# Token projections as Strassen products in a phase of their own

## The chip, the cores and the metric

The kernel runs on one core of a Trainium2 chip. The metric is the device time of one execution in microseconds; less is better.

## The reference

One layer of a gated encoder over two groups of tokens, 256 and 2048, 2304 in all, of width 1024. Normalised tokens go through one wide product with w_in; three branches (pooling, Fourier, attention into 256 memory tokens) are gated, projected, merged and projected once more.

```python
xn = rmsnorm(x, norm_in[l])
mn = rmsnorm(mem, norm_mem[l])
pv, pg, fv, fg, q, ag, mg = split_cols(xn @ w_in[l])
ya = (pool_mixer(pv, w_pool_grp[l], pool_scale[l]) * jax.nn.silu(pg)) @ w_pool_out[l]
yb = (fourier_mixer(fv, w_four_grp[l]) * jax.nn.silu(fg)) @ w_four_out[l]
yc = (memory_xattn(q, mn, w_kv[l]) * jax.nn.silu(ag)) @ w_attn_out[l]
ga, gb, gc = jnp.split(jax.nn.sigmoid(mg + b_gate[l]), N_BRANCH, axis=-1)
merged = ga * ya + gb * yb + gc * yc
x = x + merged @ w_o[l]
```

The pooling mixer takes, for each of four groups of features, the mean over a window of 2, 4, 8 or 16 tokens less the token itself. All is float32.

## The kernel before

Every product is made of three matmuls (SPLITS): each float32 operand is split into a high part (a cast on ACT, L88) and a low part (a subtraction on DVE, L89), and high x high, high x low and low x high are added in PSUM. A weight tile (128 features wide) is loaded as raw by the SP queue and split into hl; four raw and three hl buffers.

Features lie on partitions, tokens along the free dimension. The 2304 tokens are three blocks of 768, a block two halves of 384. First a phase normalises and transposes the tokens (nine chunks of 256), writes them split to DRAM (xs_d), folds w_pool into w_in, and computes the Fourier values pfv; then come the Fourier mixer along tokens, and keys and values of the memory (pv L607, pk L625, stored to kv_d). From 266 us on the main pass goes block by block. It holds the block's split tokens in eight xn tiles, loaded on the POOL queue (L587), and runs in this order on PE:

- pF: the eight tiles of q and ag, with the four heads' attention woven between their matmuls: scores ps, softmax on DVE and ACT (L724 to L732), transposes pt, values po.
- for each of eight output tiles a gate pgc and yc's product pyc, then pfg (four), then pgb and pyb in turn; a gate's sigmoid is on ACT, its multiplication on DVE, and the addition of branch b to partial on POOL (L846).
- ppv and ppg in turn for eight tiles: a pooling value goes to a buffer U, DVE adds shifted copies (L872, L876), corrects the sequence's edges (L881), scales and subtracts (L882), multiplies by the gate (L891) and splits za. Two tiles have each of the four windows.
- pga and pya in turn (L664 is the one matmul line of all these), the sum in partial, its split m, and the output projection pwo (L936) with the residual and the final normalisation (L941, L946).

Each token projection (pF, pfg, ppv, ppg and the three gates: 52 tiles of a block) is 8 x 3 x 2 = 48 matmuls. A projection's closing work on ACT and DVE runs while PE does the next one. In the last block the last tile of the output is closed in two halves. Order on an engine is the order in which a timing model of the framework placed the instructions; POOL's order is the order of the code.

## Time and profile before

| | |
|---|---|
| time, median of 3 runs | 2257.05 us (2256.16 to 2260.65) |
| the profiled execution, its span | 2258.0 us |
| PE busy | 2230.9 us, 99% |
| DVE, ACT, POOL busy | 39%, 29%, 8% |
| main pass | 266 to 2250 us |
| bytes moved | 249.49 MB, 110 GB/s on the mean |

The span runs from the first to the last instruction. Matmuls overlap, so that their busy time adds up to more than the time they take; the chain that ended last shows the time of a run of them. The granted clock is TensorE's share of its full 2.4 GHz.

### The profile page before, as it was taken

Reading aid. Unit: us, or ns where it says so; the run is one execution under the profiler, and the core shown is the slowest. Engines: PE = TensorE matmul, PEld = TensorE weight load, DVE = VectorE, ACT = ScalarE, POOL = GpSimd, SP = SyncE. Lnnn points to the kernel's source line nnn. Section 1 sums busy time; section 2 is a strip of 40 time slices with the busy share of each in tenths; the row PEclk is TensorE's granted clock in tenths of the full one; section 3 lists DMA queues with packets and bytes.
Section 4 is the critical chain, followed back from the end, with each engine's and each line's share of the span. In section 5 each row is a group of like instructions: output and inputs, shape, how many; then the busy total and the mean of one; then the engine's idle time right before and its main releaser. Section 6 shows DMA issues by size and latency. Waiting matters only on the chain.

```text
span 2258.0 us, 30415 instructions
## 1 busy us (share of the span) xinstructions
PE 2230.9 (99%) x13023; PEld 2182.3 (97%) x13023; DVE 886.8 (39%) x1203; ACT 663.6 (29%) x953; POOL 191.5 (8%) x259
## 2 busy tenths in 40 slices
PE   8998999999999999999999999999999999999998
PEld 7998899999999998999999999998999999999996
DVE  6638352223345225552232344235642222343243
ACT  5433252131223114442222222123441222222131
POOL 1226210001100000100012100000000012000000
PEclk9999999999999999999999999999999999999999
DMA  9986931222222225711322222227412312122221
GB/s 327 344 219 226 291 101 52 70 85 66 75 64 67 66 66 195 241 47 57 96 64 68 77 66 57 65 93 259 144 47 66 94 57 83 57 66 62 60 103 75
DMA packets 295338, 249.49 MB, mean 110 GB/s; under 512 B 8644, under 2 KB 264164, under 8 KB 294948
## 3 DMA queue, kind: packets, MB, share of 16 engines
q1 hardware_dynamic: 243552, 171.47, 25.1%
q0 software_dynamic: 50880, 74.20, 11.3%
q8 instruction: 102, 1.67, 0.3%
q10 hardware_dynamic: 772, 1.88, 0.3%
q14 instruction: 32, 0.26, 0.0%
HBM read 201.91 MB, written 45.61 MB: 110 GB/s over the span
## 4 chain that ended last, share of the span: by engine, by line
PE 97%; DVE 1%; DMA 1%; issue 0%; ACT 0%; POOL 0%; SPq 0%; DVEq 0%; ACTq 0%
PE ppv L664 9%; PE ppg L664 9%; PE pgc L664 9%; PE pgb L664 9%; PE pga L664 9%; PE pF L664 9%; PE pya L664 9%; PE pwo L936 9%; PE pfv L316 5%; PE pfg L664 4%; PE pyb L664 4%; PE pyc L664 4%; PE po L756 1%; PE ps L714 1%; PE pv L607 1%; PE pk L625 1%
## 5 line engine op out<-in xcount | busy, mean ns | idle before, releaser
L89 DVE TENSOR_TENSOR hl<-raw,hl 128x1024 fp32r<-128x1024 f32 (+1 forms) x270 | 316.3, 1172 | 589.3 <-ACT hl L88 583.1
L88 ACT CAST hl<-raw 128x1024 fp32r<-128x1024 f32 (+1 forms) x270 | 261.8, 970 | 369.1 <-PE pya L664 136.9
L664 PE MATMUL pF<-xn,hl 128*128 128x384 f32 x1152 | 211.6, 339 | 0.0
L664 PE MATMUL ppv<-xn,hl 128*128 128x392 f32 (+2 forms) x1152 | 208.3, 340 | 0.0
L664 PE MATMUL ppg<-xn,hl 128*128 128x384 f32 x1152 | 205.9, 337 | 0.0
L664 PE MATMUL pgb<-xn,hl 128*128 128x384 f32 x1152 | 205.8, 337 | 0.0
L664 PE MATMUL pgc<-xn,hl 128*128 128x384 f32 x1152 | 205.8, 337 | 0.0
L664 PE MATMUL pga<-xn,hl 128*128 128x384 f32 x1152 | 205.8, 337 | 0.0
L664 PEld LDWEIGHTS ppv<-xn,hl 128*128 128x128 f32 x1152 | 204.6, 188 | 0.0
L664 PE MATMUL pya<-za,hl 128*128 128x384 f32 x1152 | 203.3, 334 | 0.0
L664 PEld LDWEIGHTS ppg<-xn,hl 128*128 128x128 f32 x1152 | 202.3, 188 | 0.0
L664 PEld LDWEIGHTS pgb<-xn,hl 128*128 128x128 f32 x1152 | 202.2, 188 | 0.0
L664 PEld LDWEIGHTS pgc<-xn,hl 128*128 128x128 f32 x1152 | 202.2, 188 | 0.0
L664 PEld LDWEIGHTS pga<-xn,hl 128*128 128x128 f32 x1152 | 202.2, 188 | 0.0
L664 PEld LDWEIGHTS pF<-xn,hl 128*128 128x128 f32 x1152 | 201.1, 188 | 0.3
L664 PEld LDWEIGHTS pya<-za,hl 128*128 128x128 f32 x1152 | 200.3, 188 | 0.0
L936 PE MATMUL pwo<-hl,m 128*128 128x512 f32 x648 | 148.2, 389 | 0.0
L936 PEld LDWEIGHTS pwo<-hl,m 128*128 128x128 f32 x648 | 121.6, 188 | 25.3
L846 POOL TENSOR_TENSOR partial<-partial,gb 128x768 f32<-128x768 f32 x24 | 62.3, 2595 | 766.7 <-ACT hl L88 515.8
L316 PE MATMUL pfv<-xhi,fvw 128*128 128x256 f32 x576 | 107.7, 287 | 0.0
L664 PE MATMUL pyb<-zb,hl 128*128 128x384 f32 x576 | 104.0, 335 | 0.0
L664 PE MATMUL pyc<-zc,hl 128*128 128x384 f32 x576 | 103.9, 335 | 0.0
(240 smaller groups left out, 2364.5 us busy)
## 6 DMA issues: line engine op xcount, KB each, us to landing
raw<-in_w_in_dram SPq DMA_DIRECT2D x136, 512.0 KB, 3.9
raw<-in_w_o_dram SPq DMA_DIRECT2D x40, 512.0 KB, 3.4
xn<-xs_d POOLq DMA_DIRECT2D x16, 776.0 KB, 11.6
...
```

What stands on the lines that cost most here:

```text
L88: nc.scalar.copy(hi, src)
L89: nc.vector.tensor_sub(lo, src, hi.bitcast(F32))
L316: nc.tensor.matmul(o, lhsT=fvw[:, g, a, d * P:(d + 1) * P], rhs=hl[b][:, d, :], start=(d == 0 and s == 0), stop=(d == 7 and s == 2))
L607: nc.tensor.matmul(pv[m // 2][:, m % 2, :], lhsT=mn(a, d)[:, m * P:(m + 1) * P], rhs=w[:, c, k * 512:(k + 1) * 512], start=(d == 0 and s = ...
L625: nc.tensor.matmul(ps[:, 0, :], lhsT=w[:, a, d * P:(d + 1) * P], rhs=mn(c, d), start=(d == 0 and s == 0), stop=(d == 7 and s == 2))
L664: nc.tensor.matmul(ps[:, j, :n], lhsT=w[:, a, d * P:(d + 1) * P], rhs=rhs(c, d, c0, n), start=(d == 0 and s == 0), stop=(d == nd - 1 and s ...
L714: nc.tensor.matmul(flat(ps)[:, t * 256:(t + 1) * 256], lhsT=qT[h][:, a, tt * P:(tt + 1) * P], rhs=kload[h, req(tt)][:, c, :], start=(s == ...
L756: nc.tensor.matmul(ps[:, hf, c0:c0 + n], lhsT=vload[h, r][:, a, m, :], rhs=z[:, c, m * H + c0:m * H + c0 + n], start=(m == 0 and s == 0), ...
L846: nc.gpsimd.tensor_add(partial[:, c, :], partial[:, c, :], sg[:, :TB])
L936: nc.tensor.matmul(ps[:, hf, :], lhsT=m[d][:, a, lc:lc + P], rhs=w[:, cc, hf * 512:(hf + 1) * 512], start=(d == 0 and (a, cc) == (0, 0)), ...
```

## The change

The 52 projection tiles of a block are taken two at a time. A pair of 128-feature tiles and the two halves of the 1024 inputs make a 2 x 2 matrix of weight blocks (A11 to A22); the 256 tokens of a chunk are two groups of 128, so that the tokens make 2 x 2 blocks too. Seven products of sums of such blocks replace the eight of the plain form. A product has 4 x 3 matmuls of 384 columns, in which the moving operand is 128 tokens from each of three chunks.

The seven token operands of a block (xo0 to xo6, 1.57 MB each with both parts) are read from DRAM (xq_d) on the POOL queue. For the first block's three chunks the normalising phase makes them (x_sums); for the other six it stores the transposed tokens (xr_d), and x_prep makes them within the first phase, in pairs 6, 12 and 18 of blocks 0 and 1. Each operand has one buffer: at the last pair of a block it is loaded anew after its last product. Weight sums S1 to S4 are made on DVE, split, and kept in ten buffers; PE's order is written by hand, preparing eight products ahead.

All results (q, ag, fg, pv, pg and the gates, after silu or sigmoid) are stored to DRAM on the POOL queue, two of 0.39 MB per pair. When all three blocks are done, a second phase goes over the blocks again and loads them on the SP queue into five shared buffers (ld_tile). It begins with the attention of block 0; attention of the next block is taken into the loop over ya. The closing of the last tile in halves is dropped, and every block loads w_o twice.

```diff
+    pairs = [((wp_d, c * P, "pv", c), (wp_d, (c + 4) * P, "pv", c + 4)) for c in range(4)]
+    pairs += [((w_in, Q0 + h * P, "q", h), (w_in, AG0 + h * P, "ag", h)) for h in range(4)]
+    pairs += [((w_in, FG0 + g * P, "fg", g), (w_in, FG0 + (g + 2) * P, "fg", g + 2)) for g in range(2)]
+    pairs += [((w_in, PG0 + c * P, "pg", c), (w_in, PG0 + (c + 4) * P, "pg", c + 4)) for c in range(4)]
+    for k in (2, 1, 0):
+        pairs += [((w_in, MG0 + 1024 * k + c * P, "g", 8 * k + c), (w_in, MG0 + 1024 * k + (c + 4) * P, "g", 8 * k + c + 4))
+                  for c in range(4)]
+    e_pair = [[[st.add(ftile(w, c0)) for w, c0, _, _ in pr] for pr in pairs] for _ in range(NB)]
...
+    def x_sums(x, ta, tb):
+        x11, x21, x12, x22 = x
+        V.tensor_sub(ta[:, 0], x12, x11)
+        V.tensor_sub(ta[:, 1], x22, ta[:, 0])
+        V.tensor_sub(tb[:, 0], x22, x12)
+        V.tensor_sub(tb[:, 1], x21, ta[:, 1])
...
+            if c >= 3:
+                nc.gpsimd.dma_start(xr_d[c - 3][:, j * D:(j + 1) * D], r)
+        if c < 3:
+            nc.gpsimd.dma_start(xq_d[c][:, 0:2, :], xc[:, 0].rearrange("p h a f -> p h (a f)"))
+            nc.gpsimd.dma_start(xq_d[c][:, 2, :], xc[:, 1, 1].rearrange("p a f -> p (a f)"))
+            ts = [temp(f"xt{ci}_{k}").rearrange("p (o f) -> p o f", o=2) for k in range(2)]
+            x_sums(quarters(src), *ts)
+            for k in range(2):
+                hl = hl_tile(f"xth{ci}_{k}").rearrange("p o (a f) -> p o a f", a=2)
+                split(hl[:, :, 0, :], hl[:, :, 1, :], ts[k])
+                nc.gpsimd.dma_start(xq_d[c][:, 3 + 2 * k:5 + 2 * k, :], hl.rearrange("p o a f -> p o (a f)"))
...
-    def load_xn_piece(xn, b, d):
-        lo, hi = x_cols(b)
-        nc.gpsimd.dma_start(xn[d][:, :, :hi - lo], xs_d[:, d * P:(d + 1) * P, lo:hi].rearrange("a p t -> p a t"))
-
+    XOPS = (0, 5, 2, 4, 6, 1, 3)
+    xop = {}
+    def load_xop(pool, b, o):
+        t = pool.tile([P, 3, 2, 4, P], F32R, tag=f"xo{o}", name=f"xo{b}_{o}")
+        nc.gpsimd.dma_start(t.rearrange("p c a d t -> p c (a d t)"),
+                            xq_d[3 * b:3 * b + 3].rearrange("c p o f -> p c o f")[:, :, o, :])
+        xop[o] = t
...
+    PROD = {1: ("x", "A11", 0, True), 6: ("x", "S2", 4, False), 5: ("x", "S1", 3, False), 3: ("x", "S4", 2, False),
+            2: ("y", "A12", 1, True), 7: ("z", "S3", 5, True), 4: ("z", "A22", 6, False)}
+    ORDER = ((0, 1), (0, 7), (-1, 3), (0, 6), (-1, 4), (0, 2), (0, 5))
...
+        def mm(self, p):
+            tag, op, xo, first = PROD[p]
+            if first:
+                self.ps[tag] = psg.tile([P, 512], F32, tag=f"g{tag}", name=f"g{tag}_{self.nm}",
+                                        bufs=2 if tag == "y" else 3)
+            o = self.ps[tag][:, :384]
+            w, x = self.ops.pop(op), xop[xo]
+            for d in range(4):
+                for s, (a, c) in enumerate(SPLITS):
+                    nc.tensor.matmul(o, lhsT=w[:, a, d * P:(d + 1) * P], rhs=x[:, :, c, d, :],
+                                     start=(first and d == 0 and s == 0), stop=(d == 3 and s == 2),
+                                     skip_group_check=True)
...
+        def store(self, k):
+            _, _, kind, idx = pairs[self.i][k]
+            nc.gpsimd.dma_start(DST[kind][idx][:, self.b * TB:(self.b + 1) * TB],
+                                self.out[k].rearrange("p c j t -> p (c j t)"))
...
+            o0, o1 = self.out
+            if p == 1:
+                self.s1 = self.keep("s1")
+            elif p == 6:
+                self.u2 = self.keep("u2")
+            elif p == 5:
+                u4 = self.keep("u4")
+                V.tensor_add(o1[:, :, 1, :], v(u4), v(self.ps["z"]))
+            elif p == 2:
+                V.tensor_add(o0[:, :, 0, :], v(self.s1), v(self.ps["y"]))
+            elif p == 3:
+                self.act(0, o0[:, :, 1, :], v(self.ps["x"]))
+                if pairs[self.i][0][2] in FUNC:
+                    self.act(0, o0[:, :, 0, :], o0[:, :, 0, :])
+                self.store(0)
+            elif p == 4:
+                V.tensor_add(o1[:, :, 0, :], v(self.u2), v(self.ps["z"]))
+                if pairs[self.i][1][2] in FUNC:
+                    self.act(1, o1, o1)
+                self.store(1)
+    def x_prep(c):
+        src = []
+        for j in range(2):
+            t = temp(f"xl{c}_{j}")
+            nc.gpsimd.dma_start(t, xr_d[c - 3][:, j * D:(j + 1) * D])
+            src.append(t.rearrange("p (d t) -> p d t", d=8))
+        x = quarters(src)
+        ts = [temp(f"xt{c}_{k}").rearrange("p (o f) -> p o f", o=2) for k in range(2)]
+        x_sums(x, *ts)
+        for o, v in enumerate((x[0], x[1], x[3], ts[0][:, 0], ts[0][:, 1], ts[1][:, 0], ts[1][:, 1])):
+            hl = la.tile([P, 2, 512], F32R, tag="wop", name=f"xp{c}_{o}", bufs=10)
+            split(hl[:, 0, :], hl[:, 1, :], v)
+            nc.gpsimd.dma_start(xq_d[c][:, o, :], hl.rearrange("p a f -> p (a f)"))
+    plist = [Pair(b, i) for b in range(NB) for i in range(len(pairs))]
+    seq = []
+    for n in range(len(plist) + 1):
+        for dn, p in ORDER:
+            if 0 <= n + dn < len(plist):
+                seq.append((plist[n + dn], p))
+    AHEAD = 8
+    with tc.manual_schedule(engines={mybir.EngineType.PE}):
+        for k in range(-AHEAD, len(seq)):
+            if k + AHEAD < len(seq):
+                q, p = seq[k + AHEAD]
+                q.prep(PROD[p][1])
+            if k < 0:
+                continue
+            q, p = seq[k]
+            q.mm(p)
+            q.post(p)
+            if p == 5 and q.b + 1 < NB and q.i in (6, 12, 18):
+                x_prep(3 * (q.b + 1) + (6, 12, 18).index(q.i))
+            if q.i == len(pairs) - 1 and q.b + 1 < NB:
+                o = PROD[p][2]
+                load_xop(x_pool(o), q.b + 1, o)
...
+    def ld_tile(name):
+        return lb.tile([P, 800], F32, tag="ld", name=name, bufs=5)
...
+        def step(self, i):
+            if i == 0:
+                self.load(0)
+                self.q_split(0)
+            if 1 <= i - 1 < 5:
+                self.values(i - 2)
+            if 0 <= i - 1 < 4:
+                self.turn(i - 1)
+                self.load_v(i - 1)
+            if 0 <= i < 4:
+                self.scores(i)
+                if i + 1 < 4:
+                    self.load(i + 1)
+                    self.q_split(i + 1)
+    at = Attention(0)
+    for i in range(6):
+        at.step(i)
+    for b in range(NB):
+        e = eb[b]
+        class Loads:
+            def __init__(self, todo, ahead=3):
+                self.todo, self.ahead, self.done = todo, ahead, []
+            def get(self, i):
+                while len(self.done) <= min(i + self.ahead, len(self.todo) - 1):
+                    k = len(self.done)
+                    self.done.append(self.todo[k](k))
+                return self.done[i]
+        def gates(k):
+            return Loads([lambda c, k=k, b=b: load_cols(g_d[8 * k + c], f"g{k}_{b}_{c}", b) for c in range(8)])
...
-            sg = sig(1, c, proj(e["gb"][c], xrhs, 8, CH, f"pgb{b}_{c}"), f"gb{b}_{c}")
-            ps = proj(e["yb"][c], y_rhs(zb), 4, ZC, f"pyb{b}_{c}")
+            sg = lg.get(c)
+            ps = proj(e["yb"][c], y_rhs(zb), 4, f"pyb{b}_{c}")
...
+        lu = Loads([load_u] * 8, 1)
...
-            ps = proj(e["pv"][c], xrhs, 8, PCH, f"ppv{b}_{c}")
+            U, sg = lu.get(c)
...
-        for c in range(7):
-            sg = sig(0, c, proj(e["ga"][c], xrhs, 8, CH, f"pga{b}_{c}"), f"ga{b}_{c}")
-            merge(c, sg, proj(e["ya"][c], y_rhs(za), 8, ZC, f"pya{b}_{c}"))
-        py = proj(e["ya"][7], y_rhs(za), 8, ZC, f"pya{b}_7")
-        pg = proj(e["ga"][7], xrhs, 8, CH, f"pga{b}_7")
-        for c in range(7):
+        lg = gates(0)
+        nxt = Attention(b + 1) if b < NB - 1 else None
+        for c in range(8):
+            sg = lg.get(c)
+            ps = proj(e["ya"][c], y_rhs(za), 8, f"pya{b}_{c}")
+            if nxt and c < 6:
+                nxt.step(c)
+            merge(c, sg, ps)
+        for c in range(8):
             m_split(c)
-        merge(7, sig(0, 7, pg, f"ga{b}_7"), py)
-        m_split(7)
-
-        # ---- output projection, residual, final RMSNorm
+        at = nxt
...
-            if last and gr == 1:
...
-                for hf in range(2):
-                    cols = slice(hf * 512, (hf + 1) * 512)
...
-                continue
```

On PE, at the end of yb in block 0. Before, pooling values ppv (on x tiles xn) follow:
```order
L664 MATMUL pyb0_7_5439<-zb0_0_4569,hl94_5346 128x384 x6
L664 MATMUL pyb0_7_5439<-zb0_1_4635,hl94_5346 128x384 x6
L664 MATMUL pyb0_7_5439<-zb0_2_4697,hl94_5346 128x384 x6
L664 MATMUL pyb0_7_5439<-zb0_3_4759,hl94_5346 128x384 x6
L664 MATMUL ppv0_0_5471<-xn0_0_2634,hl95_5378 128x392
L664 MATMUL ppv0_0_5471<-xn0_0_2634,hl95_5378 128x384
```
After, ya (pya) follows, whose operand za comes out of the pooling sums:
```order
L852 MATMUL pyb0_7_14701<-zb0_3_14453,hl222_14632 128x384 x6
L852 MATMUL pya0_0_14909<-za0_0_14750,hl223_14664 128x384 x6
L852 MATMUL pya0_0_14909<-za0_1_14768,hl223_14664 128x384 x6
L852 MATMUL pya0_0_14909<-za0_2_14788,hl223_14664 128x384 x6
L852 MATMUL pya0_0_14909<-za0_3_14808,hl223_14664 128x384 x6
L852 MATMUL pya0_0_14909<-za0_4_14830,hl223_14664 128x384 x6
L852 MATMUL pya0_0_14909<-za0_5_14852,hl223_14664 128x384 x6
L852 MATMUL pya0_0_14909<-za0_6_14876,hl223_14664 128x384 x6
L852 MATMUL pya0_0_14909<-za0_7_14893,hl223_14664 128x384 x6
L897 MATMUL ps1_0_0_14965<-k1_0_1_14958,q1_0_14962 128x256 x2
```
ppv and ppg have gone to the first phase; pya of tile 0 stands next to yb, tile by tile of za, and the scores ps1 of block 1's attention behind it.

On DVE at the same place. Before, the multiplication by yb's last product and the first sums:
```order
L845 TENSOR_TENSOR gb0_6_5344<-gb0_6_5344,pyb0_6_5351 128x768
L89 TENSOR_TENSOR hl95_5378<-raw95_5205,hl95_5378 128x1024
L89 TENSOR_TENSOR hl96_5434<-raw96_5261,hl96_5434 128x1024
L845 TENSOR_TENSOR gb0_7_5432<-gb0_7_5432,pyb0_7_5439 128x768
L89 TENSOR_TENSOR hl97_5466<-raw97_5293,hl97_5466 128x1024
L872 TENSOR_TENSOR s2_0_0_5526<-U0_0_5520 128x791
L89 TENSOR_TENSOR hl98_5532<-raw98_5349,hl98_5532 128x1024
L881 TENSOR_TENSOR s2_0_0_5526<-s2_0_0_5526,edge_77 128x8 x3
L882 SCALAR_TENSOR_TENSOR s2_0_0_5526<-s2_0_0_5526,U0_0_5520 128x776
```
After:
```order
L1020 TENSOR_TENSOR g1_0_6_14564<-g1_0_6_14564,pyb0_6_14669 128x768
L97 TENSOR_TENSOR hl224_14696<-raw224_14569,hl224_14696 128x1024
L1020 TENSOR_TENSOR g1_0_7_14598<-g1_0_7_14598,pyb0_7_14701 128x768
L97 TENSOR_TENSOR hl225_14904<-raw225_14603,hl225_14904 128x1024
L1047 TENSOR_TENSOR s2_0_0_14742<-U0_0_14728 128x791
L1056 TENSOR_TENSOR s2_0_0_14742<-s2_0_0_14742,edge_84 128x8 x3
L1047 TENSOR_TENSOR s2_0_1_14760<-U0_1_14735 128x791
L1057 SCALAR_TENSOR_TENSOR s2_0_0_14742<-s2_0_0_14742,U0_0_14728 128x776
```
In both the sums s2 stand behind the multiplication that waits for yb's last tile pyb0_7; in after the next sums follow each other directly where before weight splits (hl) stood between them.

On PE, the first attention. Before, scores (ps) of head 0 stand among the products pF:
```order
L664 MATMUL pF0_1_3016<-xn0_3_2637,hl52_2903 128x384 x6
L664 MATMUL pF0_1_3016<-xn0_4_2638,hl52_2903 128x384 x6
L664 MATMUL pF0_1_3016<-xn0_5_2639,hl52_2903 128x384 x6
L664 MATMUL pF0_1_3016<-xn0_6_2640,hl52_2903 128x384 x6
L664 MATMUL pF0_1_3016<-xn0_7_2641,hl52_2903 128x384 x6
L714 MATMUL ps0_0_0_3047<-k0_0_0_2946,q0_0_3008 128x256 x6
L714 MATMUL ps0_0_0_3047<-k0_0_1_2948,q0_0_3008 128x256 x3
L714 MATMUL ps0_0_1_3057<-k0_0_1_2948,q0_0_3008 128x256 x9
L664 MATMUL pF0_2_3125<-xn0_0_2634,hl53_2954 128x384 x6
L664 MATMUL pF0_2_3125<-xn0_1_2635,hl53_2954 128x384 x6
```
After, they follow the last product of the first phase (gz):
```order
L726 MATMUL gx_2_25_13551<-xo2_2_10269,wS4_2_25_13530 128x384 x12
L726 MATMUL gz_2_25_13568<-xo2_6_10310,wA22_2_25_13548 128x384 x12
L897 MATMUL ps0_0_0_13707<-k0_0_0_13698,q0_0_13704 128x256 x6
L897 MATMUL ps0_0_0_13707<-k0_0_1_13700,q0_0_13704 128x256 x3
L897 MATMUL ps0_0_1_13731<-k0_0_1_13700,q0_0_13704 128x256 x9
L921 MATMUL pt0_0_0_13764<-ident_79,pe0_0_0_13723 128x128 x6
L921 MATMUL pt0_0_1_13774<-ident_79,pe0_0_1_13747 128x128
```
The transposes pt, which wait for the softmax, now follow the scores directly, with no other product between.

## Rows read from the trace of the kernel before

**Rows 1.** The page: span, busy time of each engine, and the chain by engine.
```profile
span 2258.0 us, 30415 instructions
...
PE 2230.9 (99%) x13023; PEld 2182.3 (97%) x13023; DVE 886.8 (39%) x1203; ACT 663.6 (29%) x953; POOL 191.5 (8%) x259
...
PE 97%; DVE 1%; DMA 1%; issue 0%; ACT 0%; POOL 0%; SPq 0%; DVEq 0%; ACTq 0%
```

**Rows 2.** The chain in order of time: start us, us, what.
```profile
929.11 13.70 PE pF L664 x78
...
1018.73 8.43 PE pgc L664 x48
...
1253.92 8.58 PE ppv L664 x48
```

**Rows 3.** PE's groups: line, engine, operation, names, count | busy us, mean ns.
```profile
L664 PE MATMUL ppv<-xn,hl 128*128 128x392 f32 (+2 forms) x1152 | 208.3, 340 | 0.0
...
L664 PE MATMUL pgc<-xn,hl 128*128 128x384 f32 x1152 | 205.8, 337 | 0.0
...
L664 PE MATMUL pfg<-xn,hl 128*128 128x384 f32 x576 | 101.5, 337 | 0.0
```

**Rows 4.** DVE by line and form: count | busy us, mean ns | idle before.
```profile
L872 DVE TENSOR_TENSOR s<-U 128x783 f32<-128x783 f32 x16 | 15.6, 975 | 90.8 <-ACT U L870 90.8
...
L882 DVE SCALAR_TENSOR_TENSOR s<-s,U 128x768 f32<-128x768 f32 x16 | 15.3, 957 | 0.5
...
L891 DVE TENSOR_TENSOR sga<-sga,s 128x768 f32<-128x768 f32 x16 | 15.3, 959 | 61.8 <-ACT sga L886 61.8
...
L881 DVE TENSOR_TENSOR s<-s,edge 128x8 f32<-128x8 f32 x32 | 3.9, 162 | 0.4
...
L89 DVE TENSOR_TENSOR za<-sga,za 128x768 fp32r<-128x768 f32 x24 | 22.8, 952 | 0.0
...
L89 DVE TENSOR_TENSOR hl<-raw,hl 128x1024 fp32r<-128x1024 f32 x222 | 283.0, 1275 | 291.5 <-ACT hl L88 285.4
```

**Rows 5.** POOL by line and form, and the ACT cast of za.
```profile
L846 POOL TENSOR_TENSOR partial<-partial,gb 128x768 f32<-128x768 f32 x24 | 62.3, 2595 | 766.7 <-ACT hl L88 515.8 <-DVE gb L845 251.0
...
L88 ACT CAST za<-sga 128x768 fp32r<-128x768 f32 x24 | 20.1, 837 | 3.1 <-DVE sga L889 1.7
```

**Rows 6.** A head's softmax by line and form, on DVE and ACT.
```profile
L724 DVE TENSOR_REDUCE mx<-ps 128x3 f32<-128x768 f32 x24 | 22.6, 942 | 14.1 <-PE ps L714 14.1
...
L728 ACT ACTIVATE pe<-ps,nb 128x256 f32<-128x256 f32 x72 | 33.3, 472 | 28.6 <-DVE nb L725 26.0 <-issue 2.4
...
L728 ACT ACTIVATION_READ_ACCUMULATOR pe<-ps,nb 128x1 f32 x72 | 14.4, 200 | 0.0
...
L732 DVE TENSOR_SCALAR pe<-pe,rc 128x256 f32<-128x256 f32 x72 | 21.0, 349 | 0.4
```

**Rows 7.** Stretches: us, busy us of each engine, granted clock, DMA share, GB/s.
```profile
core 0: us, PE busy (x) PEld busy (x) DVE busy (x) ACT busy (x) POOL busy (x), PEclk, DMA share, GB/s
...
188.00:192.00 4.00, 0.40 (x4) 0.21 (x2) 4.00 (x3) 1.01 (x1) 3.94 (x10) 1.00 0.00 1
...
192.00:196.00 4.00, 3.21 (x15) 3.09 (x16) 3.97 (x5) 0.71 (x3) 3.98 (x7) 0.64 0.82 263
```

**Rows 8.** The same view, other stretches, the heaviest in transfers.
```profile
860.00:865.00 5.00, 5.00 (x28) 4.77 (x27) 0.23 (x1) 1.16 (x2) 0.62 (x1) 1.00 1.10 405
...
40.00:60.00 20.00, 20.00 (x173) 20.00 (x172) 14.79 (x36) 11.82 (x21) 4.72 (x6) 1.00 1.24 376
```

**Rows 9.** Transfers: queue, count, KB each, median us from issue to landing.
```profile
k<-kv_d POOLq DMA_DIRECT2D x16, 256.0 KB, 3.6
...
kv_d<-kt POOLq DMA_DIRECT2D x8, 256.0 KB, 11.7
```

**Rows 10.** DVE by line and form: closing operations of an output tile.
```profile
L941 DVE TENSOR_TENSOR xr<-xr,pwo 128x1024 f32<-128x1024 f32 x17 | 20.0, 1216 | 27.8 <-PE pwo L936 27.7
...
L946 DVE SCALAR_TENSOR_TENSOR xr<-xr,hr_r,nf 128x1024 f32<-128x1024 f32 x17 | 21.8, 1285 | 0.6
```

434 lines of the change are left out of this document (205 added, 229 removed).

## The prediction

> **What bounds the kernel now.** I read the table of busy shares and the chain that ended last first. TensorE (PE) is busy 2230.9 of the span's 2258.0 us and holds 97% of that chain [rows 1]; nothing else holds over 1%. VectorE (DVE) is busy 39%, ScalarE (ACT) 29%. So before is a row of matmuls with 27 us of holes, and everything DVE and ACT do lies beneath it. The chain in order of time then gives the price of a matmul, since busy time of overlapping matmuls does not: 48 matmuls of 384 columns take 8.43 us, 175.6 ns each, and 48 of a pooling value 8.58 us [rows 2]. The groups by line give the counts: the gate products ppg, pgb, pgc and pga, the q/ag products pF and the pooling values ppv have 1152 matmuls each, pfg has 576 [rows 3], in all 7488 matmuls that multiply tokens by w_in or the folded weights.
>
> A second reading matters more. Where PE is full, DVE's work costs nothing, but only because PE has work that doesn't need it. The pooling sums of a block run while PE computes the next ppv and ppg; a head's softmax runs while PE computes the next pF. The change takes exactly those matmuls away from beside them. So I priced what it removes, and then walked the built order of after, engine by engine, for what stands alone.
>
> **The saving.** 52 feature tiles become 26 pairs per block, of 84 matmuls (7 products x 4 x 3) where two tiles had 96: 3 x 26 x 84 = 6552. 936 fewer at 175.6 ns are 164 us; the pooling values also lose their halo columns, 24 x 7/8 x about 0.15 us = 3 us. **-167 us**, if a matmul whose moving operand is three pieces of 128 columns runs like one of 384; no row shows such an operand.
>
> A page would price this otherwise. TensorE: Matmul & The Clock Gate of the Trainium skill (Back-to-back issue gap) says that in a stream of weight loads and matmuls both set the spacing, about 81 ns at 128 columns and 131 ns at 512. An estimate between these is 115 ns at 384, by which the removed matmuls would be worth 107 us and the sum 57 us higher; [rows 2] contradict it, so the row's price is used.
>
> **Pooling, now uncovered: +114 us.** In after, ya of a block needs za[0..7], and in the built DVE order these sums stand behind the multiplication that waits for yb's last tile. Per block: 20 window additions at 0.97 us, 8 scaled subtractions and 8 gate multiplications at 0.96, 8 splits at 0.95 = 42.3 us [rows 4]. Block 0 has 24 edge corrections at 0.16 and its multiplication in two pieces, 47.4 us; block 2 has 8 corrections, 43.6 us.
> - Block 0: U's memset stands on POOL behind eight additions to partial at 2.60 us [rows 5]; the last starts after DVE's g1, 0.96 us. So the sums begin 0.96 + 2.60 + 0.2 = 3.8 us after PE has ended yb; they take 47.4 us, plus the last ACT cast 0.84 and about 2 us of late loads (five shared load buffers). Meanwhile PE can do only pya0_0, six matmuls per za: 7 x 1.05 = 7.4 us. Then it needs q of block 1, whose load waits for za0_7: 3.6 us for the nearest load, k from kv_d [rows 9], plus 0.8 us cast less 1.05 = 3.2. Idle 50 us.
> - Block 1: the first two tiles get 6.7 us done before yb ends. 0.96 + 1.27 (a weight split) + 35.6 + 0.84 + 2 - 7.4 + 3.2 = 36.5 us.
> - Block 2: three ya tiles are interleaved, so PE has 7 x 3 x 1.05 = 22 us to do: 0.96 + 1.27 + 43.6 + 0.84 + 2 - 22 + 1 = 27.7 us.
> The bounds are 100 (loads never late, additions to partial early) and 130 us (each U late by 1 us).
>
> **Attention of block 0 alone: +33 us.** Before, the section of pF with attention takes from 929.11 to 1018.73, 89.6 us; eight times 8.43 are 67.4, so attention is 22.3 us of PE [rows 2]. After, block 0's four heads stand between the phases with nothing beside them. The first k load stands on POOL behind the store of the last pair: 1.5 us for that result, two issues, 3.6 us to land = 6.5 us. In one head DVE's order is maximum 0.94, wait for three exponentials at 0.47 + 0.20, second maximum 0.94, three scalings at 0.35, wait for three exponentials, three scalings [rows 6], with two splits at 0.95, a q split and a product between: walked with its waits, 11 us per head. The last head's transposes, cast, split and product add 4. 6.5 + 44 + 4 = 54.5, less 22.3. Bounds 26 (k lands at once) and 42 us (13 us per head). The other blocks' attention goes between ya's matmuls, which cover it.
>
> **The start of the first phase: +10 us.** Two of seven x operands are loaded only when the last key tiles are in DRAM. Such a store takes 11.7 us to land at the median [rows 9]; the load of 1.57 MB takes 3.9 us at 405 GB/s, the highest rate of a stretch [rows 8]. The products that need them come at 8.5 and 10.6 us. 1.5 + 1.4 + (4 to 12) + 5 + the second load gives 6 to 16 us of idle.
>
> **The two block changes: +16 us.** The seven operands (11 MB) have one buffer each; an operand is reloaded after its last product, 2.1 us apart, and needed 12.5 to 13 us later. 11 MB at 405 GB/s are 27 us, at the 376 GB/s of the normalising phase 29 [rows 8]; a pair's 1.05 MB of weights and 0.79 MB of results in 14.75 us want 125 GB/s beside them, so some 300 are likely left, 37 us where 26 to 29 are hidden: 8 us each. Bounds 3 (340 GB/s) and 19 us (240 GB/s).
>
> **Steady first phase: +3 us.** A pair takes 14.75 us on PE. DVE: seven splits and four sums of 512 columns (half of a 1024 split, 0.64) and three result sums of 384, about 8.6 us; ACT about as much. Each of the six x_prep adds four sums and seven splits, 7.1 us: 15.7 against 14.75 in that pair, taken from eight products of lookahead (16.9 us). PE covers it; without that cover it would be 2 us each. Bounds 0 and 12.
>
> **Normalising phase: +4 us.** DVE is busy 14.79 of 20 us [rows 8]; in three of nine chunks of 14.1 us it gets four sums at 0.64 and two splits at 1.27 more: 10.4 + 5.1 = 15.5, 1.4 us over, three times. Bounds 0 and 10.
>
> **Wake-up of PE: +10 us.** After PE idles in 188 to 192, the stretch 192 to 196 shows a granted clock of 0.64 [rows 7], a mixture of 2.4 and 1.2 GHz: 0.36 x 3.2 = 1.2 us lost, at each of eight such holes. Bounds 0 and 25.
>
> **Second phase, small.** yc's and yb's weights (half a split, 0.64) and gate loads lie under 24 matmuls, 4.2 us of PE, each; the Fourier products end with yc, and PE has 6 us of pyb on the first two of them. m's splits follow ya, and wo takes m in turn. +3 us (0 to 6). The special ending on a half tile goes; after, three whole tiles have 3 additions at 1.22 and 3 multiplications at 1.29 [rows 10], 9.5 us with their small steps before the last store: +5 us (4 to 8).
>
> **Sum**, against the profiled execution: 2258 - 167 + 114 + 33 + 10 + 16 + 3 + 4 + 10 + 3 + 5 = 2289; that execution is 1 us over the median of the runs shown: **2288 us**. The bounds, added as independent, are some 36 us to either side.
>
> **Rivals.**
> 1. The transfers hide (faster). The first phase runs without a hole: operands arrive at 340 GB/s or more, key stores land in 4 us, and PE's clock stays. Then start, changes, steady phase, normalising and wake-up (43 us) are gone: 2288 - 43 = 2245. It decides once these five cost under 7 us together. For it: 405 GB/s was reached; bounds of three are zero. Against: operands and stores share the engines that gave 376 GB/s with DMA share 1.24.
> 2. The first phase is bound by transfers. At 240 GB/s the changes are 38, the start 16, the steady phase 12 us: 2288 + 22 + 6 + 9 = 2325. For it: the results of each pair and the operands share POOL's queue, and two such stores stand ahead of every reload.
> 3. The split operand costs. If three pieces of 128 columns run 5% slower, 6552 x 8.8 ns = 57 us: 2345. Nothing in the trace speaks for it or against it. The page's rule above would end there too.
> 4. All terms near their low ends at once: pooling 100, attention 26, the five of rival 1 at 32 instead of 43: 2288 - 14 - 7 - 11 = 2256, no change.
>
> **How the numbers follow.** My forecast (2262 to 2324) 0.52; rival 1 0.22; rival 2 0.13; rival 3 0.07; rival 4 0.06. A measurement here tells 0.2% (4.5 us) from no change. Faster 0.22, same 0.06, slower 0.72. The range from 2228 to 2340 leaves out half of rival 3, a third of rival 2 and the low part of rival 1.
>
> **What would show it.** In the profile of after: PE idle some 200 us in all instead of 27; PE's slices low at three places some 270 us apart in the last third, each with DVE full on the lines of the pooling sums; pya waiting for za; a stretch of some 50 us between the last pair and the first yc with PE under half; first-phase pairs at 14.75 us apart, with holes only at two block changes. I'd be wrong if pooling sums run while yb does, if the pitch of the products isn't 175 ns, or if holes recur at every pair.

## The result: slower, and by twice what was forecast

The changed kernel takes 2322.66 us (median of 4 runs, 2321.07 to 2325.39), the kernel before 2257.31 us in the same session: a ratio of 1.0287, 95% interval 1.0272 to 1.0301. The forecast was 2288 us, 31 us slower; measured are 65. The side and the range were right, the size was not. The page of the changed kernel answers [rows 1]; of section 2 the lines of PE, DVE and the clock are shown, 58 us a digit:

```profile
span 2322.0 us, 31784 instructions
...
PE 2135.9 (92%) x12087; PEld 2058.3 (89%) x12087; DVE 1415.3 (61%) x2228; ACT 953.1 (41%) x1661; POOL 293.6 (13%) x469
...
PE   6998989999999999999999999787699957999697
...
DVE  5757365765745566574555555357765676656855
...
PEclk8999999999999999999999999898699967999899
...
PE 58%; issue 14%; DVE 7%; DMA 6%; ACT 1%; POOL 1%; SPq 0%; POOLq 0%; DVEq 0%; ACTq 0%
```

PE does 936 matmuls less, and is idle for 186 us where it was idle for 27. The largest holes lie at the very start and in the last third, where DVE is fullest. The waits of PE say for what (engine, line, what ended the wait: total us, times, longest):

```profile
PE pya L852 <- ACT za L96: 54.9, 18, 9.4
PE pya L852 <- DVE za L97: 24.9, 13, 6.6
PE pt L921 <- DVE pe L910: 18.6, 11, 3.5
PE gz L726 <- DVE out L761: 12.7, 4, 3.9
PE ps L897 <- DMA k<-kv_d: 9.9, 1, 9.9
PE pfv L352 <- ACT xc L96: 8.2, 3, 4.3
...
PE gy L726 <- DMA xo<-xq_d: 6.5, 1, 6.5
```

Pooling (za) is the largest by far, as forecast; two entries were not on the forecast's list at that size: the casts xc of the normalising phase, and DVE's result sums (out) in the first phase.

Stage by stage, from the times at which PE's groups begin and end. The ideal of a stage is its matmuls at [rows 2]'s prices: 67.4 us for yc and yb together, 67.4 for ya, 22.3 for a block's attention, 1150.5 for the products (6552 x 175.6 ns).

| stage | forecast | measured |
|---|---|---|
| up to the last key tile, against before | +4 | 284.5 - 266.0 = +18.5 |
| start of the products, to the end of its last wait: 304.9 - 284.5, less 36 matmuls | +10 | +14.1 |
| two block changes (e2) | +16 | 1480.1 - 1459.5 = +20.6 |
| rest of the products (1195.6 - 1150.5, less the two rows above) | +3 | +10.4 |
| attention of block 0, 1480.1 to yb's end at 1605.0 | +33 | 124.9 - 67.4 - 22.3 = +35.2 |
| pooling, block 0 | +50 | 140.3 - 67.4 - 22.3 = +50.6 |
| pooling, block 1 | +36.5 | 211.3 - 134.8 - 22.3 = +54.2 |
| pooling, block 2 | +27.7 | 157.3 - 134.8 = +22.5 |
| end | +5 | +4.7 |
| wake-up of PE, small items of the second phase | +13 | within the rows above |

Together 230.6 - 167 = +63.6, against 64 between the two profiled spans. What follows tests these rows one at a time. Each experiment is the changed kernel with one edit, unless it says otherwise, and its ratio is to the kernel before in its own session (2257 to 2259 us).

### The profile page after: what moved, and what is told of

Same layout as the page of the kernel before. It is cut to its first block, busy times and chain, and to the rows that moved or that the text cites. A ratio compares the mean times of both kernels' runs of the same rounds, so it can differ in the third digit from the quotient of the medians.

```text
span 2322.0 us, 31784 instructions
## 1 busy us (share of the span) xinstructions
PE 2135.9 (92%) x12087; PEld 2058.3 (89%) x12087; DVE 1415.3 (61%) x2228; ACT 953.1 (41%) x1661; POOL 293.6 (13%) x469
## 3 DMA queue, kind: packets, MB, share of 16 engines
q0 software_dynamic: 57312, 174.62, 22.5%
## 4 chain that ended last, share of the span: by engine, by line
PE 58%; issue 14%; DVE 7%; DMA 6%; ACT 1%; POOL 1%; SPq 0%; POOLq 0%; DVEq 0%; ACTq 0%
PE gx L726 20%; PE gz L726 10%; PE pwo L1099 8%; PE pya L852 7%; PE gy L726 5%; DMA raw<-wp_d 3%; PE pyb L852 3%; PE pyc L852 3%; DMA fgl<-fg_d 1%; DVE s L1051 1%; PE ps L897 1%; DMA U<-pv_d 1%; DVE pgl L1060 1%; PE po L937 1%; DVE s L1047 1%
## 5 line engine op out<-in xcount | busy, mean ns | idle before, releaser
L726 PE MATMUL gx<-xo,wS 128*128 128x384 f32 x2808 | 522.3, 339 | 1.8 <-DMA xo<-xq_d 1.3
L726 PEld LDWEIGHTS gx<-xo,wS 128*128 128x128 f32 x2808 | 498.3, 188 | 3.0 <-issue 2.1
L97 DVE TENSOR_TENSOR hl<-raw,hl 128x1024 fp32r<-128x1024 f32 (+1 forms) x128 | 141.1, 1107 | 92.1 <-ACT hl L96 91.4
L726 PE MATMUL gz<-xo,wA 128*128 128x384 f32 x936 | 182.0, 344 | 12.7 <-DVE out L761 12.7
L726 PE MATMUL gy<-xo,wA 128*128 128x384 f32 x936 | 181.5, 343 | 6.5 <-DMA xo<-xq_d 6.5
L726 PE MATMUL gz<-xo,wS 128*128 128x384 f32 x936 | 179.8, 341 | 3.4 <-ACT wS L96 2.7
L726 PEld LDWEIGHTS gz<-xo,wA 128*128 128x128 f32 x936 | 169.3, 191 | 14.0 <-DVE out L761 14.0
L726 PE MATMUL gx<-xo,wA 128*128 128x384 f32 x936 | 178.3, 339 | 1.6 <-ACT wA L96 1.6
L726 PEld LDWEIGHTS gy<-xo,wA 128*128 128x128 f32 x936 | 169.8, 191 | 6.8 <-DMA xo<-xq_d 6.8
L726 PEld LDWEIGHTS gz<-xo,wS 128*128 128x128 f32 x936 | 167.4, 189 | 4.0 <-ACT wS L96 3.1
```

The lines of the kernel that those rows point to most:

```text
L97: nc.vector.tensor_sub(lo, src, hi.bitcast(F32))
L726: nc.tensor.matmul(o, lhsT=w[:, a, d * P:(d + 1) * P], rhs=x[:, :, c, d, :], start=(first and d == 0 and s == 0), stop=(d == 3 and s == 2) ...
```

## Experiments: the uncovered work of the second phase

**e3: pooling moved under the products.** The sums are made in the first phase, pv and pg being in DRAM by then, and the second only loads and splits the result.

```
+            if p == 5 and (q.b, q.i) in at_pair:      # 8 chunks a block
+                late.append(pooled(*at_pair[q.b, q.i]))   # loads, sums, gate; stored to po_d one pair later
...
-            U, sg = lu.get(c)
...
-            z_split(za[c], sg[:, :TB])
+            z_split(za[c], lp.get(c)[:, :TB])         # lp: loads of po_d
```

> The pooling sums, the edge factors and the product with the gate are made in phase 1, between the products of the pairs that follow (DVE 59% busy there), and go through DRAM; phase 2 only loads the 8 pooled tiles of a block and splits them. Theory (what was paid in phase 2 was DVE work and loads with TensorE idle, 127 us over three blocks, and phase 1 has the room): all but the splits' 5 to 10 us a block goes, 2205 to 2230 us, which is below the 2257 of the kernel before. Rival 1 (phase 1 has no room at the places that count: some 135 us of DVE work on 59% busy DVE delays operand sums): half is given back in phase 1, 2255 to 2280. Rival 2 (the block's pooling was bound by transfers, not by DVE: 8 of 16 loads remain): 2265 to 2285.

Measured: 2288.86 us, ratio 1.0136 (1.0121 to 1.0151), 34 us less than the changed kernel, where the theory asked for 92 to 117. The second phase got 75 us shorter (last product to the end: 842 to 767), but the products ended 45 us later, at 1525 us. The time is above the ranges of both rivals; in its effect it is rival 1. The cause shows in DVE's waits between 750 and 1060 us and, below them, in PE's:

```profile
DVE s L811 <- DMA U<-pv_d: 16.6, 6, 6.5
```
```profile
PE gz L727 <- ACT wS L97: 13.7, 5, 7.0
PE gz L727 <- DVE wS L98: 8.3, 8, 1.6
```

DVE works in its own order. It stood at the first sum of a chunk until U had landed, and the operand splits wS behind it came too late for PE. That is a wait, not a lack of room, and e5 was made to tell the two apart.

**e5: the same, with U requested a pair or two ahead.**

```
-            late.append(pooled(*at_pair[q.b, q.i]))
...
+            late.append(pooled(*at_pair[at], early.pop(at)))
...
+            early[todo[0]] = pool_load(*at_pair[todo[0]])   # two buffers for U
```

> As e3_pool_early (2289 us), but the raw pooling rows U of a chunk are requested one or two pairs (15 to 30 us) before its sums, in two buffers. Theory (in e3 DVE stood in its own order behind transfers of U, 16.6 us in six waits between 750 and 1060 us, and the operand splits behind it came late: TensorE waited 33 us for wS): those waits go and phase 1 ends 20 to 30 us earlier, 2259 to 2269 us. Rival (the DVE work itself, 2 to 5 us a chunk put in one place, delays the splits): less than 8 us, 2281 to 2291.

Measured: 2246.67 us, ratio 0.9939 (0.9924 to 0.9954): 42 us less than e3, more than the theory asked, and 0.6% faster than the kernel before. The stretch 750 to 1060 us in e3 and, below it, in e5 (us, busy us and count on PE, PEld, DVE, ACT, POOL; clock, DMA share, GB/s):

```profile
750.00:1060.00 310.00, 288.00 (x1585) 283.46 (x1584) 211.87 (x364) 144.77 (x262) 52.70 (x113) 0.97 0.58 188
```
```profile
750.00:1060.00 310.00, 310.00 (x1755) 309.65 (x1755) 228.98 (x392) 159.74 (x288) 54.86 (x117) 1.00 0.62 200
```

With DVE busier (229 against 212 us) PE has no hole at all: DVE at 74% costs nothing if nothing in its order waits for a transfer. So of the 127 us of pooling 76 were the price of its place; e14, below, shows where the rest went.

**e10: the additions of yb on DVE.** Pooling stays where the change put it.

```
-            nc.gpsimd.tensor_add(partial[:, c, :], partial[:, c, :], sg[:, :TB])
+            nc.vector.tensor_add(partial[:, c, :], partial[:, c, :], sg[:, :TB])
```

> The 24 additions of yb into the partial sums go from GpSimd (2.6 us each) to DVE. Theory (block 1's pooling took 54 us where 36 were forecast because DVE's work beside GpSimd's additions is stretched, 2.5 to 4 us for what takes 0.9 to 1.3, and the edge and U buffers wait behind them): 10 to 18 us less, 2304 to 2312. Rival (the late loads of U set it, and DVE only gets 24 additions of some 0.9 us more): 2318 to 2340.

Measured: 2306.76 us, ratio 1.0209 (1.0192 to 1.0226), 16 us less. In the profiles 9.3 us of that are block 1's (yc's start to the first wo: 211.3 to 202.0) and 3.4 block 2's. Giving DVE 24 more additions made it faster. Why, is seen in block 1 of the changed kernel; first POOL, then DVE (start us, duration, what, idle before):

```profile
1875.52 2.70 POOL L1021 TENSOR_TENSOR partial<-partial,g 128x768 f32<-128x768 f32 x1 [6.71 <-DVE g L1020]
1880.92 2.40 POOL L1021 TENSOR_TENSOR partial<-partial,g 128x768 f32<-128x768 f32 x1 [2.70 <-ACT hl L96]
1887.19 2.41 POOL L1021 TENSOR_TENSOR partial<-partial,g 128x768 f32<-128x768 f32 x1 [3.88 <-ACT za L96]
```
```profile
1872.56 0.97 DVE L1047 TENSOR_TENSOR s<-U 128x783 f32<-128x783 f32 x1 [5.45 <-DMA U<-pv_d]
...
1876.44 2.60 DVE L1060 SCALAR_TENSOR_TENSOR pgl<-s,vecT,pgl 128x768 f32<-128x768 f32 x1
...
1881.58 2.55 DVE L97 TENSOR_TENSOR za<-pgl,za 128x768 fp32r<-128x768 f32 x1
...
1887.86 2.82 DVE L97 TENSOR_TENSOR hl<-raw,hl 128x1024 fp32r<-128x1024 f32 x1
...
1901.68 0.97 DVE L1047 TENSOR_TENSOR s<-U 128x783 f32<-128x783 f32 x1 [4.81 <-DMA U<-pv_d]
```

Each of these three additions catches one DVE instruction that starts while it runs. The gate product takes 2.60 us (others beside it 1.00), the split za 2.55 (0.95), the split hl 2.82 (1.21), and they end 0.8, 0.8 and 1.1 us after the addition has. (The 4 us of the expectation are a line of two instructions; the longest single one takes 2.82.) Over the whole run twelve DVE instructions with both inputs in SBUF start while one of the 24 additions runs; all twelve end after it, the nine of 512 columns by 0.55 us. Each ends as if it had begun, within 0.15 us, when the addition was done. A gate's multiplication, whose one input pyb lies in PSUM, isn't held: six start during an addition and take their usual 0.95 us, as here (POOL, then DVE):

```profile
1861.37 4.41 POOL L1021 TENSOR_TENSOR partial<-partial,g 128x768 f32<-128x768 f32 x2 [1.55 <-DVE g L1020]
```
```profile
1862.09 0.95 DVE L1020 TENSOR_TENSOR g<-g,pyb 128x768 f32<-128x768 f32 x1 [0.25 <-PE pyb L852]
```

The GPSIMD Engine Reference of the Trainium skill (Specifications) says that GpSimd shares its SBUF interfaces with VectorE and contends with DVE instructions with two SBUF inputs; the twelve are of that kind, and the trace agrees. Between 1850 and 1940 us the held instructions cost DVE 7.9 us, and in e10 the eight additions cost it 7.6: DVE pays for POOL's additions what it would pay to do them itself.

The gain is another: in that stretch DVE waited 10.3 us for U in two, in e10 2.0 us. Two things could make U late, and no run separates them. POOL's addition holds a load buffer for its 2.4 us. And POOL's queue, in order, issues the next block's keys and values, eight loads, only behind its additions; in e10 they go out 67 us earlier (the changed kernel, then e10):

```profile
1889.55 1.11 POOL L875 DMA_DIRECT2D k<-kv_d  x2
```
```profile
1822.91 1.09 POOL L875 DMA_DIRECT2D k<-kv_d  x2
```

The U behind the wait of 4.81 us was requested at 1891.6 us, among those loads, and took 10.0 us to land; in e10 no U of the block took over 5.2.

Where in block 1 the 54.2 us are lost shows in the stretch from yb's end to the first scores, and in the one from there to the first wo (the changed kernel, then the first of the two in e10):

```profile
1878.00:1932.90 54.90, 20.55 (x49) 13.47 (x49) 47.31 (x49) 10.42 (x12) 9.27 (x11) 0.52 0.65 196
1932.90:2021.70 88.80, 85.11 (x504) 84.32 (x505) 54.81 (x90) 33.45 (x73) 0.00 (x0) 0.95 0.40 126
```
```profile
1878.40:1923.90 45.50, 18.93 (x48) 12.07 (x46) 42.32 (x48) 8.74 (x10) 0.00 (x0) 0.59 0.57 178
```

The first stretch holds 48 matmuls worth 8.4 us: 46.5 us are lost, in e10 37.1. The second holds 81.3 us of matmuls and takes 88.8: another 7.5 us, of which e10 gets back next to nothing (88.2).

**e6 and e4: the attention that stands alone.** e6 requests the first keys from SP and places the partial sums' buffer after attention(0)'s buffers; e4 sets yb's products beside attention(0) and puts yc behind.

```
e6 -                nc.gpsimd.dma_start(t, kv_d[r, h, :, 0:512]...)
e6 +                (nc.sync.dma_start(t.bitcast(F32), kv_d[r, h, :, 0:512]...) if (b, h) == (0, 0) else
e6 +                 nc.gpsimd.dma_start(t, kv_d[r, h, :, 0:512]...))
...
e4 -    for i in range(6):
e4 -        at.step(i)
...
e4 +            ps = proj(e["yb"][c], y_rhs(zb), 4, f"pyb{b}_{c}")
e4 +            if b == 0 and c < 6:
e4 +                at.step(c)
```

> The start of phase 2 of the changed kernel: the first keys of attention(0) are requested by SP and not by GpSimd, behind whose last stores they stood, and the buffer of the partial sums and the row of the last norm are placed after those of attention(0), so that the first loads find room that the raw weights of phase 1 leave early. Theory (the 9.9 us from the last product to the first score are this queue and this room): 6 to 10 us less, 2313 to 2317. Rival (the keys wait for nothing but the rows of q of the last pairs or the transfer itself): 2319 to 2325.

> Block 0 alone: the Fourier products (yb) come first, with the six steps of attention(0) between them, then the attention products (yc). Theory (attention(0) alone cost 35 us because softmax on DVE and ACT had no products beside it): 22 us of products cover it, 2322 less 18 to 28 is 2294 to 2304 us. Rival (the stretch is bound by the first transfers of phase 2, 9.9 us of wait for k and 7 to 9 for the others, which now also carry the Fourier and gate rows): less than 10 us, 2313 to 2322.

Measured: e6 2317.55 us, ratio 1.0258 (1.0243 to 1.0274), 5 us less, a little under the theory. e4 2324.31 us, 1.0282 (1.0265 to 1.0299), no gain: the rival. Two steps of PE at the start of phase 2 in e6, and below it its first in e4 (start us, duration, what, idle before):

```profile
1483.25 0.73 PE L895 MATMUL ps<-k,q 128*128 128x256 f32 x4 [2.38 <-ACT q L96]
...
1499.41 0.47 PE L919 MATMUL pt<-ident,pe 128*128 128x128 f32 x1 [6.69 <-DVE pe L908]
```
```profile
1496.52 4.96 PE L852 MATMUL pyb<-zb,hl 128*128 128x384 f32 x14 [16.30 <-ACT hl L96]
```

In e6 the first score stands 6.7 us earlier (1483.3 against 1490.0), but PE then waits 6.7 us for the softmax of the second half, and yc begins only 2.1 us earlier (1534.4 against 1536.4); the rest of the gain comes behind it, most of it in block 0's pooling. In e4 PE had products to do, but no weights for them until 16.3 us after the last product. The cover was there and its loads were not.

## Experiments: the first phase and the one before it

**e2 and e11: the block changes.** e2 prices them by leaving out the reloads. e11 begins a block with the pair that the block before ended with, so that its weights are there.

```
e2  -                load_xop(x_pool(o), q.b + 1, o)
e11 +    turns = [list(range(np_)), [np_ - 1] + list(range(np_ - 1)), [np_ - 2] + list(range(np_ - 2)) + [np_ - 1]]
...
e11 +                if i0 not in kept:
e11 +                    kept[i0] = st.raw(i0), st.raw(i1)
```

> The operands of blocks 1 and 2 are not loaded: all three blocks multiply with those of block 0 (14 transfers of 1.5 MB left out, the outputs of blocks 1 and 2 are wrong by that). Theory (the reloads hold up the weight transfers, which TensorE meets as waits for DVE, 12.7 us in four, and the clock sinks to 0.93 in two stretches of 50 us): both block changes together cost 20 to 25 us, so 2297 to 2302 us. Rival (only the waits for the operands themselves, 1.3 and 0.5 us, belong to the reloads; the waits for DVE are DVE's own work, the sums of the next block among it): 2316 to 2321 us.

> Blocks 1 and 2 begin with the pair that the block before ended with, whose raw weights are still there (1 MB less to load at each change, and the weights of the next pairs are requested one pair earlier); the operand reloads are as before. Theory (DVE's waits of 9.9 and 10.3 us for raw weights at each change are what TensorE meets there; e2 prices both changes at 20.8 us): 8 to 16 us less, 2307 to 2315. Rival (the reload of 11 MB itself limits; with the weights there the waits turn into waits for operands): 2319 to 2325.

Measured: e2 2303.24 us, ratio 1.0195 (1.0180 to 1.0211), 19 us less; its products end at 1459.5 us where the changed kernel's end at 1480.1. e11 2308.53 us, 1.0220 (1.0205 to 1.0235), 14 us less. In the profiles the first phase, from the last key tile to the last product, takes 1195.6 us in the changed kernel, 1185.1 in e11 and 1174.5 in e2: half of what the changes cost went with one pair's weights, and the other 4 us of e11's gain lie in the second phase. The chain in order of time through the changed kernel's first block change shows it (start us, us, what), and the bytes moved in 40 slices of 655 to 720 us:

```profile
655.11 2.12 PE gz L726 x12
...
669.95 1.05 PE gz L726 x6
...
672.15 0.63 ACT wA L96
672.80 0.70 DVE wA L97
673.52 18.29 DMA raw<-wp_d
...
696.70 14.10 DMA raw<-wp_d
710.89 0.69 DVE tb L703
```
```profile
GB/s 0 0 9 251 299 277 61 0 242 0 121 381 408 407 362 344 404 388 386 413 369 384 391 385 388 399 391 387 386 350 409 386 388 349 304 11 10 0 209 327
```

All transfers together move 344 to 413 GB/s for 37 us, near the highest rates of [rows 8]. Who gets how much of it, two lines for 676 to 701 us show (queue, kind: packets, MB, share of the 16 engines; q0 is POOL's queue, with the operands and the stored results, q1 SP's, with the weights):

```profile
q0 software_dynamic: 2138, 8.63, 91.3%
q1 hardware_dynamic: 1986, 1.01, 19.2%
```

Both moved about as many packets, but POOL's are 4.0 KB long in the mean and SP's 0.5, so that the operands' queue gets 345 GB/s and the weights' 40. PE seldom waits for operands (1.3 us in two, at both changes). But a weight tile, requested when a raw buffer comes free, now takes 18.3 and 14.1 us to land (at the median 7.2 from wp_d and 4.2 from w_in, of the same size), and DVE's sums tb, then out, then PE's gz stand behind it. In e11 the chain there holds 15.4 us of operand transfer in their place: the rate is the next bound, at half of the cost.

**e8: two pairs at a time at a change.** I tried more room for the operands first.

```
+            two = (plist[n], plist[n + 1])          # last two pairs of a block, first two of the next
+            for p in (1, 7, 6, 2, 5, 3, 4):
...
+                seq += [(q, p) for q in two]
```

> At each block change the last two pairs of a block and the first two of the next run product by product (1 of both, 7 of both, and so on), so that 12 slots of 2.12 us lie between the last use of an operand and the first of the next block's in place of 6. Theory (without reloads phase 1 was 20.8 us shorter, e2; the reload is a rate: 11 MB at the 405 GB/s of rows 860 to 865 need 27 us, the old order gave 12.7 and the new one gives 25): 12 to 19 us go, 2304 to 2311. Rival (what waits at a change are the raw weights behind the operand transfers, and two pairs at a time want twice the weights): 2318 to 2330.

Measured: 2330.52 us, ratio 1.0309 (1.0291 to 1.0328), 8 us more by the medians and 5 by the ratios, whose intervals just overlap: no gain, as the rival said, where the theory asked for 12 to 19 us less. DVE's waits between 650 and 750 us, in the changed kernel and, below it, in e8:

```profile
DVE tb L703 <- DMA raw<-wp_d: 21.8, 3, 10.3
```
```profile
DVE tb L703 <- DMA raw<-wp_d: 29.1, 4, 15.2
```

**e7: operands in one run of 384 columns.**

```
-        t = pool.tile([P, 3, 2, 4, P], ...)
+        t = pool.tile([P, 8, 3, P], ...)            # x[:, 4 * c + d, :, :] is 384 columns in a row
```

> The operands of the products stand so that the 384 columns of a product are one run, not three runs of 128 with 4 KB between them; their transfers write runs of 512 bytes in place of 4 KB, three a piece. Theory (the three runs cost 1 to 1.5 ns of 175.5 a product): between 305 and 650 us 100 us hold 570 products (175.5 ns each) in place of 568 (176.1), which is 4 to 10 us over phase 1, while start and block changes get dearer. Rival (the pitch of 176 to 177 ns is that of any product with 384 columns): the same count, and the time is 2322 plus the dearer transfers.

Measured: 2351.4 us, ratio 1.0410 (1.0389 to 1.0431). The question was the pitch; the stretch 350 to 450 us of the changed kernel, and below it of e7:

```profile
350.00:450.00 100.00, 100.00 (x568) 100.00 (x567) 64.56 (x107) 49.62 (x90) 11.86 (x22) 1.00 0.54 171
```
```profile
350.00:450.00 100.00, 100.00 (x568) 100.00 (x567) 64.88 (x108) 48.13 (x87) 11.86 (x22) 1.00 0.53 169
```

568 matmuls in 100 us in both. (Two of them only reach into the stretch; the pitch is that of the chain shown above, 2.12 us for 12, 176.7 ns, and in e7 too 12 start every 2.12 us.) Three pieces of 128 columns cost nothing, which settles the forecast's third rival and the condition of its first term. The 29 us are the transfers in runs of 512 bytes: PE's waits for operands rise from 7.8 to 38.3 us, at the start and at the two changes.

**e1, e9, e12, e13: the normalising phase.** It grew by 18.5 us where 4 were forecast. e1 puts the split ahead of ACT's copy, e9 makes the copy on GpSimd, e12 leaves the copies out, e13 the copies and the sums.

```
e1  -            nc.scalar.copy(r, ps...)      (now behind split(xc...))
e9  +            nc.gpsimd.tensor_add(r..., xc[:, j, :, 0, :]..., xc[:, j, :, 1, :]...)
e12 +            r = xn[j]
e13 -            x_sums(quarters(src), *ts)
```

> In the normalising phase the split of a half chunk (hi cast on ACT, lo difference on DVE) is written ahead of ACT's extra copy of the same half. Theory (the queue order, not the amount of work): in the changed kernel TensorE waited 12.9 us for the casts xc (8.2 on ACT, 3.8 on DVE, 0.9 for the sums of squares) because each cast stands behind a copy of 1.02 us and behind the sums; with the cast first 8 to 13 us go: 2309 to 2314 us against 2322. Rival (the added copies and sums themselves fill ACT and DVE there): the waits only change their name, 2319 to 2325.

> In the normalising phase ACT's 18 extra copies (1.02 us each) are left out; the row copies r are made on GpSimd as hi plus lo. e1 showed that the order of copy and cast does not decide (2330 us). Theory (the copies' time on ACT, 18 us in a section of 139 us that was 124 us before, is the added work that counts): 8 to 15 us less, 2307 to 2314. Rival (DVE's sums and splits count, or GpSimd's additions stretch DVE's work beside them): 2320 to 2335.

> The 18 copies r of the transposed rows on ACT are left out and nothing takes their place (what is spilled and summed is the row before its transposition, the same bytes; the outputs are wrong by that). If ACT's copies are the cost of the normalising phase: 8 to 15 us less, 2308 to 2315. If DVE's sums and splits or the order that the scheduler gives the section are: 2319 to 2328.

> As e12_no_copy, and DVE's 12 sums of the first three chunks with their 6 splits are left out too (the stored operands of block 0 are other values; the outputs are wrong by that). If the added work is the cost: all of the 14.6 us that the section of the Fourier values grew goes, and most of the 18.5, 2303 to 2310. If e12 is already there, the same as e12. If neither moves, the cost is not the added work: above 2317.

Measured: e1 2329.71 us, ratio 1.0314 (1.0299 to 1.0329); e9 2326.99, 1.0297 (1.0282 to 1.0313); e12 2315.45, 1.0253 (1.0238 to 1.0268); e13 2303.98, 1.0204 (1.0187 to 1.0222). My first theory, the order on ACT, fell with e1, which came out above its rival's range too; the second, the engine, with e9, where the waits for xc shrank and 8.4 us for a norm took their place. e12 and e13 give the price. By the medians the copies cost 7 us and the sums with their splits another 11.5; by the end of the stage it is 10.4 and 7.1. How it divides is thus open to some 4 us, but together they are 17.5 to 18.7, nearly all of the 18.5. The matmuls of the memory keys, the last before the products, in the changed kernel, in e12 and in e13 (min, median, max ns; first and last start us):

```profile
L653 PE MATMUL pk<-mn,hl x96: 388/389/504, 256.0 to 284.1; 128*128 128x512 f32 x96
```
```profile
L652 PE MATMUL pk<-mn,hl x96: 388/389/499, 245.6 to 273.7; 128*128 128x512 f32 x96
```
```profile
L648 PE MATMUL pk<-mn,hl x96: 388/389/504, 238.5 to 266.6; 128*128 128x512 f32 x96
```

e13 ends this stage at 267.0 us, the kernel before at 266.0. Neither DVE nor ACT is full there (37 and 31 of 50 us at most, in stretches of 50 us), so it is not the throughput of one engine; which link of the chain cast, difference, transposition, norm lengthens is not shown.

## A version that beats both

**e14** joins e5, e6, e10 and e11, and requests the next block's first queries ahead of the pooled tiles (in e5 PE waited 10.5 and 9.7 us for them). **e15** adds e4's order, now that the loads are early.

> e5 (pooling in phase 1), e6 (start of phase 2), e10 (additions on DVE) and e11 (same weights at a change) together, and the next block's first queries requested before the pooled tiles (in e5 TensorE waited 10.5 and 9.7 us for them). If the causes add up: 2247 less 5 (e6), 0 to 8 (e10, whose pooling has gone), 8 to 16 (e11) and 15 to 20 (queries) is 2198 to 2219 us. If they share one cause (transfers or DVE in phase 2): 2225 to 2245.

> e14 (2191 us) with the order of e4 in block 0: the first scores, then the Fourier products with the other steps of attention(0) between them, then the attention products. In e14 attention(0) stands alone from 1471 to 1526 us for 22.3 us of products, 33 us over. Theory (e4 failed because its weights and rows came late; the loads are early now): 12 to 25 us less, 2166 to 2179. Rival (the chain of softmax is as long beside products, and the weights and Fourier rows still come after the end of phase 1): 2186 to 2195.

Measured: e14 2191.25 us, ratio 0.9709 (0.9692 to 0.9726); e15 2182.03 us, 0.9665 (0.9649 to 0.9681), 3.3% faster than the kernel before. In e14 the causes add up, and a little more: 131 us less than the changed kernel, where the parts gave 104 to 125. From yc's start to the first wo, block 1 takes 161.1 us for 157.1 us of matmuls and block 2 133.4 for 134.8, where pooling had added 54 and 22: next to nothing of it is left. Two stretches of e14's second phase:

```profile
1600.00:1800.00 200.00, 197.16 (x1079) 184.84 (x1078) 127.05 (x195) 75.08 (x133) 7.46 (x14) 1.00 0.56 184
1800.00:2000.00 200.00, 196.94 (x1084) 184.98 (x1083) 132.37 (x196) 77.79 (x134) 3.20 (x6) 1.00 0.57 190
```

e15 gave 9 us, less than its theory (12 to 25) and more than its rival: PE still waits 10.5 us for its first weights behind the first scores.

```profile
1486.08 1.01 PE L916 MATMUL pyb<-zb,hl 128*128 128x384 f32 x2 [10.53 <-ACT hl L97]
```

## Why the forecast was right on the side and wrong on the size

Its signs came: PE idle for 186 us (some 200 were forecast), three low places in the last third, each with DVE nearly full, pairs 14.84 us apart (14.75). Two of its terms were far too small. (Its bounds, added as independent, come to some 35 us above and 22 below, not 36 to either side.)

- **The saving** (167 us) held but for 7 us: a matmul of the products runs at 176.7 ns, forecast 175.6, over 6552 of them. Its one condition, the split operand, holds (e7); where the 1.1 ns come from no run here shows.
- **Pooling uncovered** was the right mechanism. The step that failed is block 1's, 36.5 us against 54.2, and it failed in two places. First, the sums came later: the hole behind yb costs 46.5 us where 36.5 were forecast. It gave late loads 2 us, and DVE waited 10.3 us for U. The forecast had POOL's additions in block 0, as something to wait for before a memset, but nowhere as something that holds DVE's instructions, load buffers and POOL's queue. e10, which takes the additions from POOL, has this hole at 37.1 us. Second, 7.5 us are lost behind the hole, where the forecast took the next block's attention to be covered by ya: PE waits 3.7 us for its softmax, and the granted clock is 0.95 in the mean.
- **Blocks 0 and 2** came out near (50.6 for 50, 22.5 for 27.7), block 0 by luck. Its hole costs 44.9 us, 5 less than forecast, and 5.6 us lie behind it as in block 1. The hole is shorter because the durations of DVE's instructions were added up: 76 of them in a row there, 48.5 us long in all, take 45.2 us with 2.3 us of waits, since the next starts up to 0.1 us before one ends. The forecast saw this of PE's matmuls and not of DVE.
- **Attention alone**, 33 against 35.2: right. The first score came 9.9 us after the last product (6.5 forecast), the four heads with the end took 46.4 us (48).
- **The normalising phase** is the second step that failed: 4 us against 18.5. It compared the work of a chunk with its time on DVE alone and charged only the excess, and ACT's copies nothing. The bounds, 0 to 10, did not hold it. Without the added work e13 ends the stage 17.5 us earlier, though neither DVE nor ACT was full.
- **The start** (10 against 14.1) and **the changes** (16 against 20.6) lay inside their bounds. For the changes that is luck, for the cause was wrong: the forecast asked when the operands arrive, and what arrives late are the weights beside them. With 340 GB/s it would have forecast 3 us a change; POOL's queue got 345, and PE idles all the same.
- **The rest of the first phase** is 10.4 us against 3, inside its bounds, for another reason than the forecast's: in the pairs with x_prep PE waits for nothing. 7 us are the pitch, and 2.4 the 24 matmuls behind the start's last wait, at a granted clock of 0.63.
- **The wake-up** (10) is no row of its own: those 2.4 us belong to it, and some 3 and 4 us behind the holes of blocks 0 and 1.
- **The rivals.** Rival 1 (transfers hide) fails at four of its five places, and the fifth, the clock, is contained in them; rival 2 gives nearly the time that was measured, 2325, by a mechanism that isn't there (the operands' queue got 345 GB/s, not 240, and the changes cost 20.6 us, not 38); rival 3 falls with e7.

Block 1 and the normalising phase are 32 of the 34 us by which the forecast was short; the smaller misses nearly cancel.
